# Queries and keys of the second head group as one product of quarters: seven jobs of 256 tokens

## The chip, the cores and the metric

One core of a Trainium2 chip runs the whole kernel as one program. The time is device microseconds of one execution. The engines are TensorE (PE; the loading of its weights is listed as PEld), VectorE (DVE), ScalarE (ACT), GpSimd (POOL) and SyncE (SP), whose queue issues nearly all DMAs. Each engine has its own stream of instructions; semaphores order the streams against each other.

## The reference

One layer of a decoder trunk on 512 tokens of width 1024, all in float32. After a norm, `u` is multiplied with one wide matrix `w_in` and split:

```python
u = rmsnorm(x, ln1_g[i])
proj = u @ w_in[i]
q, k, v, pool_in, z, xbc, dt_raw, gate_pre = jnp.split(proj, split_idx, axis=-1)
...
y_a = dilated_attention_mixer(q, k, v, rel_bias) @ w_a[i]
y_b = pool_mixer(pool_in, pool_w[i], pool_scale[i]) @ w_b[i]
y_c = ssd_mixer(z, xbc, dt_raw, ...) @ w_c[i]
gates = jax.nn.sigmoid(gate_pre + b_gate[i]).reshape(b, s, N_BRANCH, D_MODEL)
merged = gates[:, :, 0] * y_a + gates[:, :, 1] * y_b + gates[:, :, 2] * y_c
```

A gated feed-forward part and a last norm follow. The 18 attention heads of 64 columns are in three groups of six with dilations 1, 4 and 16, so queries and keys of one group are 384 columns each. The change concerns the queries and keys of the second group (group 1 in the code): `u` (512 x 1024) times a 1024 x 768 part of `w_in`.

## The kernel before

**Products in three parts.** A float32 factor is split into a high part (a cast to fp32r on ScalarE, `cast`, L195) and a low part (the difference to it on VectorE, `lows`, L215). `mm3` (L234) adds three products in PSUM: high x high, high x low, low x high. `uh` and `ul` are the parts of `u`, laid out with the 1024 inner columns on 8 x 128 partitions and the 512 tokens along the free axis.

**Jobs.** All work on TensorE is a list of `Job`s that `program()` yields in order. A job has one piece of weights and a body that issues its matmuls. While job n is issued, `prepare` puts the low part of job n+1's weights on VectorE, the cast of job n+2's on ScalarE (in two halves, each put in by the next `step()` of a body) and the load of job n+3's on SP's queue. There are two buffers for loaded weights (`wraw`), three for high parts (`whp`), two for low parts (`wlp`). The order of TensorE, ScalarE, VectorE and GpSimd is the order in which the code issues; SP's queue is ordered by the scheduler. `step()` also moves side work on: items of attention, of the scan and of the splits that wait in lists, one piece per step.

**PSUM.** Eight tiles of 128 x 512 float32, four under `MM`, four under `SM`, given out in turn.

**Products of quarters.** `sevens` and `sevens_down` compute a 2 x 2 block product with seven block products in place of eight, on sums and differences of quarters. `v_pair` (used for the values of groups 1 and 2) takes `u` by halves of the tokens and by even and odd inner blocks (`side_u`, with sums made by `sums_of_u`), and the weights by even and odd inner blocks and by left and right 384 columns. Its jobs have 24 matmuls of 384 columns (L234, tile `pb`), two tiles per job, each read out by an operation of its own. Differences of weights are made on VectorE by `diff` (L339), either after a job's low part (`then`) or just ahead of its cast (`form`).

**Queries and keys.** `qk_jobs(g)` has three jobs of 48 matmuls, each with 128 query and 128 key columns; a chunk is 24 matmuls of 512 tokens into a fresh `pqk` tile. ScalarE reads the query tile (L639), VectorE the key tile (L641).

**Order around the change.** `program()` runs `v_pair`, with the second branch's gate jobs 0 to 3 ahead of it, then `qk_jobs(1)`, then puts the attention items of group 1 on the list (`attend(1)`), then the gate chunks 4 to 7 (`SPLIT` is 4; two chunks of 24 matmuls per job, tile `pa`; the sigmoid is at L1085, the product at L1087), then the twelve chunks of xBC (L830, L834). The values' quarters are written to their places by 32 small DMAs on SP (L624).

Of the kernel before, what the change touches and what calls it, by code (L numbers as in the profile page):

```python
# [10 lines left out]
F32 = mybir.dt.float32  # L11
F32R = mybir.dt.float32r
AF = mybir.ActivationFunctionType
OP = mybir.AluOpType
AX = mybir.AxisListType

P = 128
S = 512
# [14 lines left out]
C_Q, C_K, C_V = 0, AW, 2 * AW  # L33
# [50 lines left out]
def trunk(ctx: ExitStack, tc, out, x, rel_bias, ln1_g, w_in, b_gate, w_a, pool_w, pool_scale, w_b,  # L84
# [3 lines left out]
    act, dve, pool, pe, sp = nc.scalar, nc.vector, nc.gpsimd, nc.tensor, nc.sync  # L88

    x, w_in, w_a, w_b, w_c, w_o = x[0], w_in[0], w_a[0], w_b[0], w_c[0], w_o[0]  # L90
# [10 lines left out]
    ypool = ctx.enter_context(tc.tile_pool(name="ypool", bufs=2))  # L101
# [6 lines left out]
    def T(name, dt=F32, shape=(P, S)):  # L108
        return big.tile(list(shape), dt, name=name, tag="t")

    def MM(name):
        return psum.tile([P, S], F32, name=name, tag="mm")
# [15 lines left out]
    def fill(items):  # L128

        for it in items:  # L130
            at = next((i for i, w in enumerate(waiting) if w is FREE), None)
            if at is None:
                waiting.append(it)
            else:
                waiting[at] = it
# [3 lines left out]
    def flush():  # L139
        todo = second[:]  # L140
        second.clear()
        for f in todo:
            f()
# [6 lines left out]
    def advance(it, phase):  # L150
        for at in it:
            if at is None or at > phase:
                return at
        running.remove(it)

    def step():
        flush()
        if waiting:
            running.append(iter(waiting.pop(0)))
        now = [(it, 0) for it in running]  # L160
        for phase in (0, ROWS, WHOLE):
            now = [(it, advance(it, phase) if at == phase else at) for it, at in now]

    def after(n, it):
        for _ in range(n):
            yield
        yield from it
# [57 lines left out]
    def wsrc(w, k0, k1, c0, c1):  # L225
        return w[k0 * P:k1 * P, c0:c1].rearrange("(k p) c -> p k c", p=P)

    def mm3(ps, wh, wl, xh, xl, ks, first=True, last=True, flip=False, again=False):

        n, total = 0, 3 * len(ks)  # L230
        for a, b in ((wh, xh), (wh, xl), (wl, xh)):
            for k in ks:
                l, r = (b(k), a(k)) if flip else (a(k), b(k))
                pe.matmul(ps, l, r, start=first and n == 0, stop=last and n == total - 1,  # L234
                          skip_group_check=again)
                n += 1

    def chunk_a(ps, ws, j, xh, xl, ks, lo=0, hi=S, k0=0):
        wh, wl = ws
        mm3(ps[:, lo:hi], lambda k: wh[:, k0 + k, j * P:(j + 1) * P],  # L240
            lambda k: wl[:, k0 + k, j * P:(j + 1) * P],
            lambda k: xh(k)[:, lo:hi], lambda k: xl(k)[:, lo:hi], ks)

    def chunk_a2(ps, ws, j, xh, xl):

        wh, wl = ws
        for k0 in (0, 4):
            mm3(ps, lambda k: wh[:, k, j * P:(j + 1) * P], lambda k: wl[:, k, j * P:(j + 1) * P],
                xh, xl, range(k0, k0 + 4), k0 == 0, k0 == 4)
            if k0 == 0:  # L250
                step()
# [86 lines left out]
    def diff(out, a, b):  # L338
        dve.tensor_tensor(out, a, b, OP.subtract)  # L339
        return out  # L340
# [70 lines left out]
    def side_u(j):  # L411
        if j in QUARTER:
            two, half = QUARTER[j]
            return [(uh[:, 2 * p + two, half], ul[:, 2 * p + two, half]) for p in range(4)]
        return [US[j, p] for p in range(4)]
# [151 lines left out]
    def perm(ap, g):  # L567
        return ap if g == 0 else ap.rearrange("p (j r) -> p r j", r=4)

    def grouped(ap, g):  # L570

        return ap.rearrange("p (r j) -> p r j", r=4)[:, :, ::-1]

    def blocked(ap, g):
        return ap.rearrange("p (r j) -> p r j", r=4) if g == 0 else perm(ap, g)

    def plain(ap, g):
        return ap if g == 0 else ap.rearrange("p (r j) -> p r j", r=4)

    dtr = cpool.tile([P, 4, SH], F32, name="dtr")  # L580
    V, QK, OT, NM, LS = {}, {}, {}, {}, {}
# [46 lines left out]
    def qk_jobs(g):  # L628
        for i in range(3):
            def body(ws, i=i):  # L630
                for j, which in enumerate("qk"):
                    ps = MM("pqk")
                    if g == 2 and i >= 3 - MORE:
                        chunk_a2(ps, ws, j, uhk, ulk)
                    else:
                        chunk_a(ps, ws, j, uhk, ulk, range(KD))
                    t = T(f"{which}{g}")
                    if which == "q":
                        act.mul(grouped(t, g), blocked(ps, g), 0.125)  # L639
                    else:  # L640
                        dve.tensor_copy(plain(t, g), perm(ps, g))  # L641
                    QK[which, g, i] = t
                    step()
            cq, ck = C_Q + 384 * g + i * P, C_K + 384 * g + i * P
            yield Job([wsrc(w_in, 0, KD, cq, cq + P), wsrc(w_in, 0, KD, ck, ck + P)], KD, 256, body)

    def attend(g):
        nm, ls = both[:, :, :HEADS], both[:, :, 32:]
# [172 lines left out]
    XS, YT, Y = {}, {}, {}  # L821
# [259 lines left out]
    def gate_jobs(b, lo=0, hi=8):  # L1081
        def evac(m, ps):
            s = SG[b, lo + m] = T("sg")
            o = o_bg + 8 * b + lo + m
            act.activation(s, ps, AF.Sigmoid, bias=col[:, o:o + 1])  # L1085
            if b == 1:
                dve.tensor_tensor(MG[lo + m], MG[lo + m], s, OP.mult)  # L1087

        return jobs_a(w_in, C_GATE + b * D + lo * P, hi - lo, uhk, ulk, KD, evac)
# [305 lines left out]
    def program():  # L1395
        yield from jobs_a(w_in, C_POOL, 8, uhk, ulk, KD, pool_evac)
        yield Call(lambda: waiting.append(rows_of_bias()))
        yield from v_jobs(0)
        yield from qk_jobs(0)
        yield from pool_out_job()  # L1400
        yield Call(lambda: attend(0))
        yield Call(lambda: waiting.insert(3, ssd_prep()))
        for i, job in enumerate(branch_jobs(1, w_b, YB, 8, more=range(7))):
            if i == 3:
                yield Call(lambda: running.extend(after(p, sums_of_u(p)) for p in range(4)))
            yield job
        load, pair = v_pair()
        yield Call(load)
        yield from gate_jobs(1, 0, SPLIT)
        yield from pair  # L1410
        yield from qk_jobs(1)
        yield Call(lambda: attend(1))
        yield from gate_jobs(1, SPLIT)
        yield from jobs_a(w_in, C_XBC, 12, uhk, ulk, KD, xbc_evac)
        yield Call(ssd_start)
        yield from qk_jobs(2)
        yield Call(lambda: attend(2))
        yield Call(lambda: fill([after(2, combine())]))
        yield from gate_jobs(0)
        many = {"a": branch_jobs(0, w_a, AO, 3), "g": gate_jobs(2),  # L1420
                "Z": z_jobs(0), "z": z_jobs(1)}
        for token in MIX:
            if token in many:
                yield next(many[token])
            else:
                yield Call(lambda i=int(token): waiting.append(y_norm(i)))
        yield Call(finish)
        yield from branch_jobs(2, w_c, YT, 8, last=True)
        yield Call(load_x1)
        for pair in range(2):  # L1430
            for h in range(2):
                yield from wo_jobs(pair, h)
            if pair == 0:
                yield Call(ff_cols)
        first, between, _ = sevens_down(0)
        second_, last_, opened = sevens_down(1, keep=True)
        extra = {EARLY + i: between[w] for i, w in enumerate(
            ("two", "one", "five", "three", "six", "seven", "four"))}
        extra.update({LATE + i: last_[w] for i, w in enumerate(("two", "one", "five", "six"))})
        for i, job in enumerate(up_jobs()):  # L1440
            yield job
            if i == EARLY - 3:
                yield Call(first)
            if i == LATE - 1:
                yield Call(second_)
            if i in extra:
                yield extra[i]
        yield Call(lambda: fin.setdefault("g", grow(final_g)))
        yield Call(finish)
        yield from down(last_, opened)  # L1450
# [79 lines left out]
    banks = [SM("uT") for _ in range(4)]  # L1530
# [7 lines left out]
    for tb in range(2):  # L1538
        s0, s1, v, sq, r, rt = (small(n, [P, 1]) for n in ("s0", "s1", "v", "sq", "r", "rt"))
# [22 lines left out]
    parts = lows(weights[1], 2)  # L1562


    r = rstd_of(ss, 2, D)
    for tb in (2, 3):
        for h in range(2):
            t = xin[tb, h]
# [65 lines left out]
SPLIT = 4  # L1634
# [33 lines left out]
```

## Time and profile before

| | |
|---|---|
| median of 3 runs | 1036.35 us (1036.2 to 1037.03) |
| the profiled execution, its own time | 1036.32 us |
| span of the profile | 1034.5 us |
| seven value jobs of groups 1 and 2 (168 matmuls of 384) | 29.14 us |
| queries and keys of group 1 (144 matmuls of 512) | 32.68 us |
| one gate chunk (24 matmuls of 512), the first after them | 5.44 us |

The page of the profile gives the span, each engine's busy time and the granted clock of TensorE. The chain of waits is followed back from the last instruction: at each step to what released it. In its view by time each row has a start, a length, an engine, the tile it writes, a line, and a count. In the timeline, rows have a start, a length, the engine and the operation with its tiles; a bracket at the end gives idle time of the engine ahead of it and what ended that. In the views by tile and by line, durations are nanoseconds (least/median/most, or the mean).

### The profile page before, as it was taken

The page shows a single profiled execution, that of the slowest core. Times are in us where ns is not written, and L with a number is a line of the kernel's source. Part 1 is how long each engine was busy: PE and PEld are TensorE (multiplying, and loading weights), DVE is VectorE, ACT ScalarE, POOL GpSimd, SP SyncE. Part 2 cuts the span into 40 slices and gives each one's busy share as a digit, 9 for nine tenths or more (in the row PEclk, how much of TensorE's full clock was granted, in tenths as well). Part 3 has the DMA queues.
Part 4 walks back from the last instruction along what each step waited for, and adds up shares of the span by engine and source line. Part 5 has one row for each costly group of instructions (what it writes and reads, how often), then busy time and mean ns, then how long its engine had stood idle before and what let it go on. Part 6 is the DMA issues. An engine that isn't in the chain of part 4 may idle for free.

```text
span 1034.5 us, 13089 instructions
## 1 busy us (share of the span) xinstructions
PE 1024.3 (99%) x5204; PEld 859.9 (83%) x5204; DVE 676.0 (65%) x907; ACT 473.8 (46%) x765; POOL 149.2 (14%) x125
## 2 busy tenths in 40 slices
PE   9999999999999999999999999999999999999997
PEld 9998878898888878888888888898888888888885
DVE  5553566684356658766768756766778677666775
ACT  6432554452464354567455324545444443453342
POOL 2770000000000004210153501101111001111120
PEclk9999999999999999999999999999999999999999
DMA  8344312026222345541254525443223324323142
GB/s 279 124 127 139 108 55 75 31 62 203 82 82 82 88 132 127 144 133 57 76 154 139 187 82 203 167 143 123 82 92 124 111 82 163 122 82 122 61 143 82
DMA packets 119068, 120.76 MB, mean 117 GB/s; under 512 B 5315, under 2 KB 101382, under 8 KB 119007
## 3 DMA queue, kind: packets, MB, share of 16 engines
q1 hardware_dynamic: 118415, 119.07, 35.9%
q8 instruction: 41, 0.67, 0.3%
q10 hardware_dynamic: 592, 0.86, 0.2%
q14 instruction: 20, 0.16, 0.0%
HBM read 116.12 MB, written 2.22 MB: 114 GB/s over the span
## 4 chain that ended last, share of the span: by engine, by line
PE 97%; DVE 1%; ACT 1%; DMA 1%; issue 0%; ACTq 0%; DVEq 0%
PE pa L234 35%; PE pu L234 22%; PE pb L234 11%; PE pqk L234 9%; PE p L234 8%; PE pa L1519 2%; PE ps L670 1%; PE pu L1326 1%; PE ppw L234 1%; PE pt L698 1%; PE po L711 1%; PE py L996 1%; DMA xin<-in_x_dram 1%; PE pyo L1003 1%; PE pst L982 0%; PE pxs L950 0%
## 5 line engine op out<-in xcount | busy, mean ns | idle before, releaser
L215 DVE TENSOR_TENSOR wl<-raw,wh 128x2048 fp32r<-128x2048 f32 (+3 forms) x95 | 218.4, 2301 | 46.9 <-ACT wh L195 39.2
L195 ACT CAST wh<-raw 128x1024 fp32r<-128x1024 f32 (+3 forms) x188 | 189.3, 1026 | 60.7 <-DVE raw L339 29.7
L1187 DVE SCALAR_TENSOR_TENSOR hc<-pu,fcol,hc 128x510 f32<-128x510 f32 x88 | 65.8, 748 | 61.1 <-ACT hc L1184 59.5
L234 PE MATMUL pa<-uh,wh 128*128 128x512 f32 x384 | 98.5, 398 | 0.0
L234 PE MATMUL pa<-ul,wh 128*128 128x512 f32 x384 | 94.9, 389 | 0.0
L234 PE MATMUL pa<-uh,wl 128*128 128x512 f32 x384 | 94.9, 389 | 0.0
L234 PEld LDWEIGHTS pa<-ul,wh 128*128 128x128 f32 x384 | 72.1, 188 | 15.2
L234 PEld LDWEIGHTS pa<-uh,wl 128*128 128x128 f32 x384 | 72.1, 188 | 15.0
L234 PE MATMUL pu<-uh,wl 128*128 128x512 f32 (+1 forms) x352 | 83.6, 380 | 0.0
L234 PE MATMUL pu<-uh,wh 128*128 128x512 f32 (+1 forms) x352 | 83.6, 379 | 0.0
L234 PE MATMUL pu<-ul,wh 128*128 128x512 f32 (+1 forms) x352 | 83.5, 379 | 0.0
L234 PEld LDWEIGHTS pa<-uh,wh 128*128 128x128 f32 x384 | 70.3, 188 | 14.7 <-issue 0.7
L234 PEld LDWEIGHTS pu<-uh,wl 128*128 128x128 f32 x352 | 64.1, 188 | 12.7 <-DVE wl L215 0.3
L234 PEld LDWEIGHTS pu<-ul,wh 128*128 128x128 f32 x352 | 64.2, 188 | 12.5
L234 PEld LDWEIGHTS pu<-uh,wh 128*128 128x128 f32 x352 | 64.1, 188 | 12.4
L1192 POOL TENSOR_TENSOR hc<-hc 128x512 f32<-128x512 f32 x22 | 30.4, 1384 | 278.9 <-DVE hc L1187 243.9
L1184 ACT ACTIVATE hc<-pu,fcol,fcol 128x512 f32<-128x512 f32 x40 | 31.2, 780 | 82.3 <-PE pu L234 82.0
L958 POOL TENSOR_TENSOR xd<-xc,dec 128x512 f32<-128x512 f32 x6 | 6.4, 1062 | 334.1 <-DVE xc L952 334.1
L1085 ACT ACTIVATE sg<-pa,col 128x512 f32<-128x512 f32 x24 | 16.5, 688 | 55.3 <-PE pa L234 48.6
L691 ACT ACTIVATE sb<-sb,both 128x128 f32<-128x128 f32 (+1 forms) x72 | 30.1, 418 | 23.5 <-DVE both L688 13.4
L234 PE MATMUL pqk<-uh,wh 128*128 128x512 f32 x144 | 36.9, 394 | 0.0
L234 PE MATMUL pqk<-ul,wh 128*128 128x512 f32 x144 | 36.3, 389 | 0.0
(352 smaller groups left out, 1793.5 us busy)
## 6 DMA issues: line engine op xcount, KB each, us to landing
raw<-in_w_in_dram SPq DMA_DIRECT2D x25, 1024.0 KB
raw<-in_ffn_w_up_dram SPq DMA_DIRECT2D x22, 1024.0 KB
raw<-in_ffn_w_down_dram SPq DMA_DIRECT2D x11, 1024.0 KB
raw<-in_w_in_dram SPq DMA_DIRECT2D x20, 512.0 KB
raw<-in_w_o_dram SPq DMA_DIRECT2D x8, 1024.0 KB
raw<-in_w_b_dram SPq DMA_DIRECT2D x4, 1024.0 KB
al<-ad SPq DMA_DIRECT2D x16, 256.0 KB
w<-in_ffn_w_down_dram SPq DMA_DIRECT2D x4, 1024.0 KB
```

What stands on the lines that cost most here:

```text
L195: act.copy(job.high[:, :, o], job.raw[:, :, o])
L215: (eng or dve).tensor_tensor(l[:, :, o], job.raw[:, :, o], h[:, :, o].bitcast(F32), OP.subtract)
L234: pe.matmul(ps, l, r, start=first and n == 0, stop=last and n == total - 1, skip_group_check=again)
L670: pe.matmul(pss[i][:, o:o + w * P], q[r, n * P:(n + 1) * P], k[r, kb * P:(kb + w) * P], start=True, stop=True)
L691: act.activation(sb[:, off:off + w * P], sb[:, off:off + w * P], AF.Exp, bias=nm[:, n, h:h + 1], accum_out=ls[:, n, h:h + 1])
L698: pe.transpose(pt[:, o:o + P], sb[:, o:o + P], eye)
L711: pe.matmul(po[DH * hh:DH * hh + DH, n * P:(n + 1) * P], V[g, kb + i][:, (2 * cc + hh) * DH:(2 * cc + hh + 1) * DH], probs[2 * cc + hh, mb ...
L1085: act.activation(s, ps, AF.Sigmoid, bias=col[:, o:o + 1])
L1184: act.activation(t, ps, AF.Identity, bias=ff["c1"][:, ff["b"] + m:ff["b"] + m + 1], scale=fw(2, m))
L1187: dve.scalar_tensor_tensor(t[:, sh:], ps[:, :S - sh], fw(k, m), t[:, sh:], OP.mult, OP.add)
L1192: pool.tensor_tensor(a, a, t, OP.mult)
L1519: pe.matmul(first[2 * n + j][:, lo:hi], a[:, k, j * P:(j + 1) * P], b[:, k, lo:hi], start=a is wh and b is uh and k == 0, stop=a is wl and ...
```

## The change

The three jobs of `qk_jobs(1)` go, and seven jobs of `qk_sevens(1)` come. The tokens are taken by halves of 256, the inner blocks by even and odd, and the columns by queries (h = 0) and keys (h = 1). Each job has three blocks of 128 columns; a block is 12 matmuls of 256 tokens. `at` puts block 0 and block 1 of a job in the two halves of one PSUM tile and block 2 in another. Sums of products are added in PSUM where they can be: p3 is added to p5's tiles (Z), and p6, p7 and p4 are added to p1's (X). After p6, after p7 and after p4 a part of the result is read out of X; p2 has tiles of its own (Y). `keep` copies p1 (times 0.125) and p5 aside, since they are needed later.

Six loads of 768 KB (128 x 4 x 384) replace three of 1024 KB: W[0] and W[1] stay in the two `xs` buffers, the others come through `wraw`, two of them twice. Four differences of weights (L339's `diff`) are made on VectorE. The sums of `u` made for `v_pair` are used again, so they are held longer.

In `program()` the loads of W are called after the sixth value job, gate chunks 4 and 5 come ahead of the queries and keys, and chunks 6 and 7 stay behind `attend(1)`.

```diff
@@ -643,6 +643,84 @@
                     step()
             cq, ck = C_Q + 384 * g + i * P, C_K + 384 * g + i * P
             yield Job([wsrc(w_in, 0, KD, cq, cq + P), wsrc(w_in, 0, KD, ck, ck + P)], KD, 256, body)
+
+    def qk_sevens(g):
+
+        cols = (C_Q + 384 * g, C_K + 384 * g)
+        q = lambda two, h: w_in[:, cols[h]:cols[h] + 384].rearrange(
+            "(k two p) c -> two p k c", two=2, p=P)[two]
+        W, X, Z, Y, r1, r5 = [], {}, {}, {}, {}, {}
+
+        def load():
+            for h in range(2):
+                W.append(ypool.tile([P, 4, S], F32, name="w3", tag="xs")[:, :, :384])
+                sp.dma_start(W[h], q(h, 1))
+
+        def at(banks, c):
+            return banks[c // 2][:, (c % 2) * 256:(c % 2) * 256 + 256]
+
+        def half(which, c, hi):
+            if (which, g, c) not in QK:
+                QK[which, g, c] = T(f"{which}{g}")
+            t = QK[which, g, c]
+            t = grouped(t, g) if which == "q" else plain(t, g)
+            return t[:, :, 64 * hi:64 * hi + 64]
+
+        def turned_(ap):
+            return ap.rearrange("p (j r) -> p r j", r=4)
+
+        def job(source, j, banks, name, use, form=None):
+            def body(ws):
+                wh, wl = ws
+                parts = side_u(j)
+                for c in range(3):
+                    fresh = name is not None
+                    if fresh and c % 2 == 0:
+                        banks[c // 2] = (MM if banks is Y else SM)(name)
+                    cs = slice(c * P, (c + 1) * P)
+                    mm3(at(banks, c), lambda k: wh[:, k, cs], lambda k: wl[:, k, cs],
+                        lambda k: parts[k][0], lambda k: parts[k][1], range(4),
+                        fresh and c % 2 == 0, True, again=not fresh or c % 2 == 1)
+                    use(c)
+                    if c != 1:
+                        step()
+            new = Job([source] if source is not None else [], 4, 384, body)
+            new.form = form
+            if source is None:
+                new.load = lambda: None
+            return new
+
+        def keep(r, name, banks, scale):
+            def use(c):
+                r[c] = T(name)[:, :256]
+                act.mul(r[c], at(banks, c), scale)
+            return use
+
+        def p2(c):
+            dve.scalar_tensor_tensor(half("q", c, 0), turned_(at(Y, c)), 0.125, turned_(r1[c]),
+                                     OP.mult, OP.add)
+
+        def p6(c):
+            r = T("r2")[:, :256]
+            act.copy(r, at(X, c))
+            dve.tensor_tensor(half("k", c, 0), turned_(at(Z, c)), turned_(r), OP.add)
+
+        def p7(c):
+            dve.tensor_tensor(half("k", c, 1), turned_(at(X, c)), turned_(r5[c]), OP.add)
+
+        def p4(c):
+            act.mul(half("q", c, 1), turned_(at(X, c)), 0.125)
+
+        one = job(q(0, 0), "A11", X, "p1", keep(r1, "r1", X, 0.125))
+        one.then = lambda: diff(W[0], W[0], one.raw)
+        two = job(q(1, 0), "A12", Y, "p2", p2)
+        five = job(None, 1, Z, "p5", keep(r5, "r5", Z, 1.0), lambda: W[0])
+        three = job(None, 4, Z, None, lambda c: None, lambda: W[1])
+        three.then = lambda: diff(W[1], W[1], W[0])
+        six = job(None, 2, X, None, p6, lambda: W[1])
+        seven = job(q(0, 0), 3, X, None, p7, lambda: diff(seven.raw, W[1], seven.raw))
+        four = job(q(1, 0), "A22", X, None, p4, lambda: diff(four.raw, four.raw, W[1]))
+        return load, [one, two, five, three, six, seven, four]
 
     def attend(g):
         nm, ls = both[:, :, :HEADS], both[:, :, 32:]
@@ -1407,10 +1485,15 @@
         load, pair = v_pair()
         yield Call(load)
         yield from gate_jobs(1, 0, SPLIT)
-        yield from pair
-        yield from qk_jobs(1)
+        load, keys = qk_sevens(1)
+        for i, job in enumerate(pair):
+            yield job
+            if i == 5:
+                yield Call(load)
+        yield from gate_jobs(1, SPLIT, SPLIT + 2)
+        yield from keys
         yield Call(lambda: attend(1))
-        yield from gate_jobs(1, SPLIT)
+        yield from gate_jobs(1, SPLIT + 2)
         yield from jobs_a(w_in, C_XBC, 12, uhk, ulk, KD, xbc_evac)
         yield Call(ssd_start)
         yield from qk_jobs(2)
```

## The prediction

> **What bounds the kernel now.** I read the page first, then the chain of waits in order of time around the changed stage, then who TensorE waited for.
>
> ```profile
> span 1034.5 us, 13089 instructions
> ...
> PE 1024.3 (99%) x5204; PEld 859.9 (83%) x5204; DVE 676.0 (65%) x907; ACT 473.8 (46%) x765; POOL 149.2 (14%) x125
> ...
> PEclk9999999999999999999999999999999999999999
> ```
>
> ```profile
> 206.56 29.14 PE pb L234 x168
> 235.71 32.68 PE pqk L234 x144
> 268.39 5.44 PE pa L234 x24
> ```
>
> ```profile
> PE pa L1476 <- DVE relb L523: 1.1, 1, 1.1
> PE pcb L927 <- ACT xcv L1015: 1.0, 1, 1.0
> ```
>
> TensorE is busy 99% of the span at full clock, and its longest wait anywhere is 1.1 us. The chain runs through the stage on TensorE alone: the values (pb, the seven jobs of v_pair), then queries and keys of group 1 (pqk), then a gate job. So a microsecond of TensorE taken out of the stage is a microsecond of the end, and any wait put in is paid in full. The stage to beat is 32.68 us.
>
> ```profile
> 206.40:235.50 29.10, 29.10 (x169) 29.09 (x168) 24.33 (x25) 13.64 (x20) 0.00 (x0) 1.00 0.21 64
> 235.50:268.20 32.70, 32.70 (x146) 27.08 (x145) 10.37 (x8) 9.79 (x11) 0.00 (x0) 1.00 0.59 185
> ```
>
> These two windows (columns: length, busy time of PE, PEld, DVE, ACT, POOL, then clock, DMA share, GB/s) compare a product of quarters with a plain one. In the first, VectorE is busy 24.33 of 29.10 us, in the second 10.37 of 32.70. The change makes the second stage like the first: cover is thin there.
>
> **What it saves on TensorE.** 144 matmuls of 512 tokens become 7 jobs x 3 blocks x 12 = 252 of 256 tokens. The price of the short ones is in the start of the kernel and of the up-projection, both with a new weight tile for each matmul:
>
> ```profile
> 12.08 9.59 PE pa L1519 x80
> ...
> 25.72 11.54 PE pa L1519 x96
> ...
> 675.86 3.83 PE pu L1326 x32
> ```
>
> 9.59/80, 11.54/96 and 3.83/32 are all 0.120 us, against 32.68/144 = 0.227. So a block of 12 takes 1.44 us, the 21 blocks 30.24, and the gain is 32.68 - 30.24 = **2.44 us**. That is the ceiling: the arithmetic falls by an eighth, but a short matmul costs more than half a long one.
>
> **What it adds: a wait after nearly every block.** Blocks 0 and 1 of a job lie in the two halves of one 128x512 PSUM tile, block 2 in another. In the changed kernel's list of instructions (it holds order and waits, no times) the first matmul of block 1 waits for the engine that empties block 0, though the halves don't overlap:
>
> ```
> p2 block 1: Matmult p2<-uh,wh 128x256 [waits DVE]
> p5 block 1: Matmult p5<-sah,wh 128x256 [waits Activation]
> p1 block 0 of seven: Matmult p1<-sbh,wh 128x256 [waits Activation]
> p1 block 1 of seven: Matmult p1<-sbh,wh 128x256 [waits DVE]
> ```
>
> By counting the semaphore's steps these are p2(0), the copy r5(0), the copy r2(1) and p7(0). Before, each chunk had a tile of its own, and in v_pair each of the two pieces. Six of the seven jobs read a result out between blocks 0 and 1 (three doesn't). What one such wait costs, no row shows; its parts do:
>
> ```profile
> L1519 PE MATMUL pa<-uh,wh x64: 278/283/365, 11.8 to 34.6; 128*128 128x256 f32 x64
> ```
> ```profile
> L1506 ACT ACTIVATE uh<-uT,g x16: 467/477/521, 10.8 to 25.3; 128x256 fp32r<-128x256 f32 x16
> L1507 DVE SCALAR_TENSOR_TENSOR ul<-uT,g,uh x16: 473/476/485, 11.3 to 26.1; 128x256 fp32r<-128x256 f32 x16
> ```
> ```profile
> L368 ACT COPY r<-pb x6: 481/482/482, 208.8 to 223.3; 128x384 f32<-128x384 f32 x6
> ```
> ```profile
> L699 DVE COPY sb<-pt 128x512 f32<-128x512 f32 x9 | 6.1, 680 | 0.0
> ...
> L716 DVE COPY o<-po 128x512 f32<-128x512 f32 x3 | 3.3, 1101 | 10.3 <-PE po L711 10.3
> ```
> ```profile
> 678.27 2.28 DVE L215 TENSOR_TENSOR wl<-raw,wh 128x2048 fp32r<-128x2048 f32 x1
> ...
> 680.61 1.98 PEld L1326 LDWEIGHTS pu<-uh,wl 128*128 128x128 f32 x16 [0.28 <-DVE wl L215]
> 680.61 2.18 PE L1326 MATMUL pu<-uh,wl 128*128 128x256 f32 x16
> ```
>
> A 256-token matmul lasts 0.283 us, so the last result is there 0.283 - 0.120 = 0.16 after its slot. VectorE ended at 678.27 + 2.28 = 680.55 and TensorE went on at 680.61: 0.05 for a semaphore each way. The 16 matmuls then took 2.18 instead of the 2.08 that 15 x 0.120 + 0.283 gives: 0.10 for starting anew. Emptying 256 columns on ScalarE lies between 0.32 (two thirds of the 384-column 0.482) and 0.48 (L1506); I take 0.40. On VectorE it lies between 0.42 and 0.77 (these reads and writes step through memory, and L716 with such steps takes 1101 against 680 in L699, times 1.6); I take 0.45, near L1507. One wait is 0.16 + 0.05 + 0.40 + 0.05 + 0.10 = **0.76 us**, and six are 4.6: already more than the gain.
>
> A rule of the Trainium skill (PSUM — Partial Sum Buffer, section on bank collisions) speaks against the change in the same way: two engines must not touch one bank of a partition together, and waits are to be set by bank, not by address. No run here shows such a collision. Set by address, the timetable below without the shared-tile waits would end 0.3 us under the old stage.
>
> **What the readers stand behind.** ScalarE and VectorE take their work in order, and between the readings stand the splits of later jobs' weights:
>
> ```profile
> L195 ACT CAST wh<-raw 128x768 fp32r<-128x768 f32 x12 | 9.7, 830 | 3.6 <-DVE raw L339 3.6
> ```
> ```profile
> 209.14 1.75 DVE L215 TENSOR_TENSOR wl<-w,wh 128x1536 fp32r<-128x1536 f32 x1
> 210.81 1.75 DVE L339 TENSOR_TENSOR w<-w,w 128x1536 f32<-128x1536 f32 x1
> ```
>
> Half a cast is 0.83 us (a new one each 0.75), a low part 1.75, a difference 1.75 (a new one each 1.67). Each sum of weights costs ScalarE nothing but makes its cast wait for VectorE. I laid the seven jobs out with these numbers, t = 0 at the first matmul of one:
> - one: r1(0) ends 2.04; block 1 starts at 2.19 instead of 1.44: **0.75**. The job ends at 5.07.
> - two: on VectorE five's low part stands ahead of p2(0). It needs the second half of five's cast, which ScalarE makes after r1(2) (5.67) until 6.43; low part to 8.23, p2(0) to 8.60, block 1 at 8.74 instead of 6.51: **2.23**.
> - five: **0.75**. It ends at 16.70.
> - three adds to p5's tile and waits for r5(1). Ahead of that on ScalarE is half of six's cast, which needs W[1] - W[0]: three's low part 12.2 to 13.95, difference to 15.62, cast to 16.50, r5(1) to 16.82: **0.27**.
> - six: its copy of block 0 stands behind seven's cast, which waits for seven's difference (21.52) and ends at 23.15; the copy ends 23.47, block 1 starts at 23.62 instead of 22.73: **0.89**.
> - seven writes the same tile: block 0 waits for copy r2(1), behind half of four's cast, behind four's difference (26.62). The copy ends 27.82; start 27.97 instead of 26.50: **1.47**. Block 1 waits for p7(0), behind four's low part (30.69); it ends 31.06, start 31.21 instead of 29.41: **1.80**.
> - four: **0.75**; the stage ends at 39.17.
>
> The waits sum to 8.91, and 30.24 + 8.91 = 39.15 (rounding apart) is 6.5 us over 32.68. **Sum: +8.9 - 2.4 = +6.5.** With both readings at their low bounds the same layout gives +5.9, with both at their high ones +8.1.
>
> **The rest, edit by edit.** The gate job put ahead of the keys is the same 48 matmuls (two of the 5.44 us pieces above), no change on TensorE. Taken out of the scores of group 1 it spares ScalarE some reloads:
>
> ```profile
> L1085 ACT ACT_TABLE_LOAD x10 | 12.8, 1283 | 0.2
> ```
>
> ScalarE isn't on the chain there, so nothing is gained; without the cover, two loads of 1.28 would be at stake. The scores of group 1 then meet two more chunks of xBC and two fewer gate chunks; before, their later items ran among xBC chunks without a wait of TensorE (the waits above name none), so I take zero, at worst a wait like pcb's 1.0. The loads: six of 768 KB for three of 1024 KB, plus where SP puts them. Its list has W[0] and W[1] before the scatter of the second values, one's weights after 8 of its pieces, two's after 16.
>
> ```profile
> 234.78 1.15 SPq L183 DMA_DIRECT2D raw<-in_w_in_dram  x2
> ...
> 236.03 5.54 SPq L624 DMA_DIRECT2D vr<-v  x8
> ...
> 238.64 1.05 ACT L195 CAST wh<-raw 128x1024 fp32r<-128x1024 f32 x1 [6.41 <-DMA raw<-in_w_in_dram]
> ...
> 241.67 1.15 SPq L183 DMA_DIRECT2D raw<-in_w_in_dram  x2
> ...
> 242.93 6.88 SPq L624 DMA_DIRECT2D vr<-v  x8
> ...
> 245.64 1.05 ACT L195 CAST wh<-raw 128x1024 fp32r<-128x1024 f32 x1 [3.60 <-DMA raw<-in_w_in_dram]
> ...
> 249.34 1.05 ACT L195 CAST wh<-raw 128x1024 fp32r<-128x1024 f32 x1 [2.65 <-DMA raw<-in_w_in_dram]
> ```
>
> one's weights take the place of the load at 234.78, needed by 246.6 now (235.71 + 2 x 5.44): hidden. two's take that of 241.67. The halves were there 4.0 us and some 7 us after their issues, so between 245.6 and 249.3; I take 246, as the load is 768 KB. Its cast stands ahead of r1(0) on ScalarE, with a gate's sigmoid between: the late bound moves r1(0) and adds 3.3 us (the layout gives +9.8). What comes later has 4 us and more to spare.
>
> **Rivals.**
> 1. Only the six plain waits stay and the queues behind them clear in time: 4.6 - 2.4 = +2.1, 1038.4. For it: v_pair ran with the same splits and not one wait. Against: there nothing of TensorE hung on the readers' places. 14%.
> 2. two's weights come late: +9.8, 1046.1. 14%.
> 3. The other side: the waits of block 1 are for the second half of the weights' cast (block 1 straddles the halves), long done, and the tiles bind nothing. Then the gain is the 2.44 less what the queues leave, 1033.9 to 1036.0; it decides if block 1 starts within 0.1 of block 0's last slot. Against: p2's wait is on VectorE, which makes no such half, and the semaphore counts. 7%.
> 4. The clock falls in the gaps. At the very start some matmuls took double:
>
> ```profile
> L1476 PE MATMUL pa<-ones x38: 274/275/579, 1.1 to 7.2; 128*128 128x128 f32 x38
> ```
>
> If the 17 blocks after two's long wait ran at double price, that is 17 x 1.44 = +24 on top, 1067. Every window quoted has clock 1.00, with gaps up to 1.1. 3%. The Trainium skill (TensorE: Matmul & The Clock Gate, Part 1) halves the clock after an idle window of about 3.4 us; my longest gap stays under it, and no trace here shows such a drop after a gap.
>
> **The numbers.** The profiled execution took 1036.32 (span 1034.5 and 1.8 around it), the median of the three is 1036.35, so the two stand for each other. 1036.32 + 6.5 = **1042.8**, 62%. The range 1039.5 to 1047.0 holds the two bounds (1042.2, 1044.4) and rival 2, and leaves out 1, 3 and 4 for the most part. A difference under 0.2% (2.07 us) can't be told from none: faster 4% (half of 3), the same 10% (the other half, and half of 1, which lies on the edge), slower 86%.
>
> **What would show it.** The stage from the first p1 to the last takes about 39 us, with TensorE idle about 9: nearly 0.75 before block 1 of one, five and four, over 2 before that of two, over 1 twice in seven. Releasers are ACT for p1 and p5, DVE for p2 and seven. Matmuls stay at 0.120. I am wrong if p1 to p4 run without gaps, if the gaps are all alike (rival 1), or if DMA is named as releaser.

## The result, and the profile after

| | before | changed |
|---|---|---|
| median | 1036.58 us (1036.2 to 1038.69, 6 runs) | 1046.53 us (1043.85 to 1048.87, 6 runs) |
| the profiled execution | 1036.32 us | 1045.46 us |
| span | 1034.5 us | 1043.5 us |

The changed kernel takes 1.0094 times as long, 95% interval [1.0075, 1.0113]. The page of its profile, the rows shown of before:

```profile
span 1043.5 us, 13347 instructions
...
PE 1024.7 (98%) x5312; PEld 864.2 (83%) x5312; DVE 690.7 (66%) x921; ACT 475.1 (46%) x778; POOL 149.4 (14%) x125
...
PEclk9999999999999999999999999999999999999999
```

TensorE's busy time didn't fall: 1024.7 against 1024.3. A matmul counts as busy until its end, which lies behind its slot, and every break in the stream shows such an end; so the eight breaks of the stage hide most of the gain of its arithmetic. Its idle time rose from 1034.5 - 1024.3 = 10.2 us to 1043.5 - 1024.7 = 18.8, and these 8.6 are most of the 9.0 by which the span is longer. The view of who TensorE waited for (total, times, longest) names them; tile `p` is that of the new jobs:

```profile
PE p L234 <- ACT r L696: 2.3, 3, 1.5
PE p L234 <- DVE q L700: 2.1, 1, 2.1
PE p L234 <- DVE k L709: 1.7, 1, 1.7
PE p L234 <- ACT r L705: 1.6, 2, 1.1
...
PE p L234 <- ACT q L712: 0.5, 1, 0.5
```

All are readings of PSUM (L696 p1 and p5, L700 p2, L705 p6, L709 p7, L712 p4). No weight and no DMA is named as releaser. The timeline of TensorE shows where; these are the first four matmuls of the stage, the first four of each block that waited, and the gate job behind:

```profile
247.26 0.64 PE L234 MATMUL p<-uh,wh 128*128 128x256 f32 x4
...
250.34 0.74 PE L234 MATMUL p<-uh,wh 128*128 128x256 f32 x4 [1.49 <-ACT r L696]
...
256.97 0.74 PE L234 MATMUL p<-uh,wh 128*128 128x256 f32 x4 [2.06 <-DVE q L700]
...
262.02 0.74 PE L234 MATMUL p<-sah,wh 128*128 128x256 f32 x4 [0.47 <-ACT r L696]
...
265.49 0.74 PE L234 MATMUL p<-sbh,wh 128*128 128x256 f32 x4 [0.34 <-ACT r L696]
...
271.97 0.74 PE L234 MATMUL p<-sah,wh 128*128 128x256 f32 x4 [0.46 <-ACT r L705]
...
276.25 0.74 PE L234 MATMUL p<-sbh,wh 128*128 128x256 f32 x4 [1.15 <-ACT r L705]
...
279.63 0.74 PE L234 MATMUL p<-sbh,wh 128*128 128x256 f32 x4 [1.69 <-DVE k L709]
...
284.67 0.74 PE L234 MATMUL p<-uh,wh 128*128 128x256 f32 x4 [0.47 <-ACT q L712]
...
287.64 2.00 PE L234 MATMUL pa<-uh,wh 128*128 128x512 f32 x8
```

The eight brackets sum to 8.13 us. The stage takes 287.64 - 247.26 = 40.38 us, against 32.68 before: +7.70. A bracket counts from the end of the last matmul, so a wait is 0.16 longer in slots: block 1 of one could have started at 247.26 + 1.44 = 248.70 and started at 250.34. The rest of the span's 9.0 us lies outside: the values start at 207.36 in this execution's chain of waits, 0.8 later than before, since the first tokens' load took 6.82 us in place of 6.06; and some 0.5 come after the stage, most of it behind the last product. The time outside the span, 1045.46 - 1043.5 = 1.96 us, is 0.14 longer too.

### The profile page after: what moved, and what is told of

It reads as the page before. It is cut to its first block, busy times and chain, and to the rows that moved or that the text cites. A ratio compares the mean times of both kernels' runs of the same rounds, so it can differ in the third digit from the quotient of the medians.

```text
span 1043.5 us, 13347 instructions
## 1 busy us (share of the span) xinstructions
PE 1024.7 (98%) x5312; PEld 864.2 (83%) x5312; DVE 690.7 (66%) x921; ACT 475.1 (46%) x778; POOL 149.4 (14%) x125
## 4 chain that ended last, share of the span: by engine, by line
PE 92%; DVE 3%; ACT 2%; DMA 1%; issue 1%; SPq 1%; ACTq 0%; DVEq 0%
PE pa L234 34%; PE pu L234 22%; PE pb L234 10%; PE p L234 9%; PE pqk L234 6%; PE pa L1602 2%; PE ps L748 1%; PE pu L1404 1%; DVE wl L215 1%; PE ppw L234 1%; PE pt L776 1%; PE po L789 1%; PE py L1074 1%; DMA xin<-in_x_dram 1%; ACT wh L195 1%
## 5 line engine op out<-in xcount | busy, mean ns | idle before, releaser
L1267 ACT ACTIVATE hc<-hc 128x512 f32<-128x512 f32 x22 | 13.9, 632 | 42.7 <-DVE hc L1265 42.6
L912 DVE SCALAR_TENSOR_TENSOR xs<-pa,col,xs 128x509 f32<-128x509 f32 (+2 forms) x24 | 18.0, 749 | 17.0 <-ACT xs L908 16.5
```

Source lines behind the costliest of these rows:

```text
L912: dve.scalar_tensor_tensor(t[:, sh:], ps[:, :S - sh], col[:, o_cw + 12 * k + m:o_cw + 12 * k + m + 1], t[:, sh:], OP.mult, OP.add)
L1267: act.activation(t, t, AF.Silu)
```

## The experiments

**A tile for each block, and the order of one difference.** Three kernels ran beside one that has only the reordering. In the first, each of the 21 blocks has a PSUM tile of its own:

```diff
-            return banks[c // 2][:, (c % 2) * 256:(c % 2) * 256 + 256]
+            return banks[c][:, :256]
...
-                    if fresh and c % 2 == 0:
-                        banks[c // 2] = (MM if banks is Y else SM)(name)
+                    if fresh:
+                        banks[c] = (SM if banks is X or (banks is Y and c == 0) else MM)(name)
...
-                        fresh and c % 2 == 0, True, again=not fresh or c % 2 == 1)
+                        fresh, True, again=not fresh)
```

> Each of the 21 blocks is added up in a PSUM tile of its own (nine tiles), all else as in the changed kernel. Theory 'shared tile': block 1 no longer waits for the reading of block 0; the same layout with the durations now measured gives a stage of 32.6 us (40.4 in the changed kernel) with 2.4 us of waits left, all in front of block 1 of seven and block 0 of four, so a time within 1 us of the kernel before (about 1036.5). Rival 'work of splitting': TensorE waits because VectorE and ScalarE have too much to do in 30 us, whatever the tiles; then most of the 9 us of waits stay and the time is over 1042.

It took 1037.74 us (1037.29 to 1041.0), ratio 1.0015 [1.0006, 1.0024] to the kernel before. Seven of the eight waits are gone, with the same weights split on the same engines. Left is one, in seven, behind the cast that waits for four's difference:

```profile
PE p L234 <- ACT r L705: 1.7, 1, 1.7
```

It stands ahead of block 1 of seven; the one that I expected ahead of block 0 of four didn't come. So the shared tile made the other waits, and the rival falls. The median is 1.2 us over the 1036.5 of the layout. The profile is that of the slowest execution, 1041.0, in which the clock fell twice, once at the start of the kernel and once in the stage ("the clock" below), so it can't say where the median's 1.2 lie. In the second kernel the one wait left is taken on too: the difference for four's weights goes ahead of seven's low part on VectorE, where it had idle time.

```diff
-        four = job(q(1, 0), "A22", X, None, p4, lambda: diff(four.raw, four.raw, W[1]))
-        return load, [one, two, five, three, six, seven, four]
+        four = job(q(1, 0), "A22", X, None, p4)
+        return load, [one, two, five, three, Call(lambda: diff(four.raw, four.raw, W[1])),
+                      six, seven, four]
```

> As before it with a tile for each block, and the difference for four's weights is made on VectorE ahead of seven's low part instead of behind it (it then lies in VectorE's idle time). Theory 'shared tile plus queue order': no wait is left, the stage takes 21 x 1.44 = 30.2 us, 2.4 under the kernel before: about 1034.1. Rival 'work of splitting': VectorE still needs some 23 us of the 30 and new waits of more than 1 us show elsewhere; no faster than 1036.

The chain of waits by time, around the stage:

```profile
236.51 10.92 PE pa L234 x48
247.44 30.31 PE p L234 x252
277.75 5.47 PE pa L234 x24
```

252 matmuls in 30.31 us, TensorE alone: 21 x 1.44 = 30.24 holds, 2.37 under the old stage. The time is 1035.36 us (1035.05 to 1035.68), ratio 0.9987 [0.9978, 0.9996]: faster than the kernel before by 1.3 us, not 2.4. The third kernel has the second edit alone, with the shared tiles:

> The changed kernel with its shared tiles, only the difference for four's weights is made ahead of seven's low part. Theory: of the two waits in seven (1.3 and 1.9 us) the first nearly goes to the plain 0.7, the second stays over 0.7; the layout gives 1.0 us less than the changed kernel (about 1045.5 for its 1046.5). If the queue order were the whole cause, both would go and the time fall by over 4 us.

1044.51 us (1043.25 to 1045.33). Its stage takes 38.70 us, from 247.10 to 285.80, against 39.69 in a second profile of the changed kernel (below): 1.0 less, as laid out, but by other waits than I wrote. In the changed kernel's list block 0 of seven waits behind four's cast; here that wait is gone and block 1's has grown:

```profile
277.78 0.74 PE L234 MATMUL p<-sbh,wh 128*128 128x256 f32 x4 [2.06 <-DVE k L709]
```

The other direction of the test also holds: the queue order alone is worth 1 us of the stage, the tiles, with that order, 38.70 - 30.31 = 8.4.

**The reordering alone.** The kernel before with two gate chunks ahead of the queries and keys:

```diff
         yield from pair
+        yield from gate_jobs(1, SPLIT, SPLIT + 2)
         yield from qk_jobs(1)
         yield Call(lambda: attend(1))
-        yield from gate_jobs(1, SPLIT)
+        yield from gate_jobs(1, SPLIT + 2)
```

> The kernel before with nothing but the gate job (chunks 4 and 5) moved ahead of the queries and keys of group 1. Theory: no cost and no gain, within 0.5 us of the kernel before (1036.5). Rival 'reordering costs': the items of group 1's attention now meet more xBC chunks and TensorE waits; over 1038.

1037.13 us (1036.21 to 1039.13), ratio 1.0004 [0.9995, 1.0013]. The stage took 32.64 us there, and TensorE waited nowhere in it or behind it that it had not before.

**The changed kernel again, more time for the loads, and a longer wait.**

> The changed kernel itself once more, for the spread of its executions (1043.85 to 1048.87 in six). Theory 'clock after a gap': its gaps of TensorE (up to 2.2 us) now and then halve the clock for some 3.4 us, as one of 1.75 us did in the kernel with a tile for each block, which costs 1.7 us each time; so the executions lie in steps of about 1.7 us over some 1044 to 1045.5, and the time rises as the mean granted clock falls: 1044 to 1046 at 0.998 or 0.999, about 1047 at 0.997, 1048.8 at 0.995. Rival 'late weights': the spread is from DMAs, and the clock is the same in slow and fast executions.

1045.5 us (1043.94 to 1047.11, 5 runs), ratio 1.0087 [1.0073, 1.0101]. This profile (the execution of 1044.26) has a stage of 39.69 us, from 246.66 to 286.35. Against the first, only the first wait differs:

```profile
249.05 0.74 PE L234 MATMUL p<-uh,wh 128*128 128x256 f32 x4 [0.80 <-ACT r L696]
```

Over both sets, the five executions at a mean clock of 0.999 took 1043.85 to 1045.99, the two at 0.995 1048.69 and 1048.87; of four at 0.997 three took 1046.64 to 1047.11, and the fourth is the 1044.26, whose clock was low only behind the last products. The time does not follow the mean clock alone: this execution has a lower mean than the five and is among the shortest. Next, all four gate chunks ahead of the keys:

```diff
-        yield from gate_jobs(1, SPLIT, SPLIT + 2)
+        yield from gate_jobs(1, SPLIT)
         yield from keys
         yield Call(lambda: attend(1))
-        yield from gate_jobs(1, SPLIT + 2)
```

> The changed kernel with all four remaining gate chunks ahead of the queries and keys (not two), so the loads have 10.9 us more. Theory: the wait of block 1 of one falls from 1.6 to the plain 0.7 (two's weights are there in time, so no cast holds up the reading of p1) and nothing else changes: 1.0 us less than the changed kernel, the seven other waits as they were. Rival 'late weights are the cause of the miss and the spread': over 3 us less and a spread under 1 us.

1044.7 us (1043.01 to 1045.38): 0.8 less than the 1045.5 of the changed kernel measured beside it. The wait of block 1 of one fell to the plain one, the others stayed:

```profile
259.75 0.74 PE L234 MATMUL p<-uh,wh 128*128 128x256 f32 x4 [0.47 <-ACT r L696]
...
266.38 1.03 PE L234 MATMUL p<-uh,wh 128*128 128x256 f32 x4 [2.06 <-DVE q L700]
...
272.92 0.74 PE L234 MATMUL p<-sah,wh 128*128 128x256 f32 x4 [0.47 <-ACT r L696]
```

The five executions still spread over 2.4 us (3.2 in the changed kernel's five), so the loads alone don't make the spread. Last, five copies into an unused tile on VectorE ahead of p2(0)'s reading, in the changed kernel:

```diff
         def p2(c):
+            if c == 0:
+                junk = T("junk")
+                for _ in range(5):
+                    dve.tensor_copy(junk, uh[:, 0, :].bitcast(F32))
```

> The changed kernel with five copies of 512 columns into an unused tile on VectorE ahead of the reading of p2(0), so the wait of block 1 of two grows from 2.2 us by what the copies take (2 to 3.5 us). Theory 'clock after a gap': a gap that long always halves the clock: the windows after it show a granted clock near 0.5 for about 3.4 us, and the time rises by the longer wait and 1.7 us more. Rival: the clock stays 1.00 and the time rises by the wait alone.

1048.47 us (1047.37 to 1049.77), 3.0 over the changed kernel. The wait grew by 4.24 - 2.06 = 2.18 us. Block 1 of one waited only 0.47 in this execution, with two gate chunks ahead as in the changed kernel, where it waited 1.49 and 0.80:

```profile
257.85 1.09 PE L234 MATMUL p<-uh,wh 128*128 128x256 f32 x4 [4.24 <-DVE q L704]
...
264.39 0.74 PE L234 MATMUL p<-sah,wh 128*128 128x256 f32 x4 [0.47 <-ACT r L696]
```

**The clock.** The windows of these kernels (length, busy times of PE, PEld, DVE, ACT, POOL, granted clock, DMA) have these rows below 1.00 ahead of the last product. First the kernel with a tile for each block, in the execution of 1041.0. It has two drops. One is at the start, behind a gap of 1.86 us that ended at 11.25: the transposes of the first tokens waited for a load of 7.30 us (6.06 in the profile before), and they and the 80 matmuls behind them took 3.23 and 10.00 us in place of 2.05 and 9.59, 1.6 more. The change touches nothing there. The other is behind the one gap of the stage, 1.75 us, that ended at 274.27:

```profile
10.00:12.00 2.00, 0.75 (x6) 0.75 (x7) 0.96 (x5) 2.00 (x3) 0.81 (x1) 0.97 1.08 393
12.00:14.00 2.00, 2.00 (x11) 2.00 (x11) 0.97 (x2) 1.28 (x4) 2.00 (x2) 0.50 1.05 396
14.00:16.00 2.00, 2.00 (x14) 2.00 (x13) 1.45 (x4) 1.62 (x6) 1.91 (x1) 0.68 0.35 106
...
274.00:276.00 2.00, 1.73 (x9) 1.73 (x10) 1.75 (x3) 1.23 (x3) 0.00 (x0) 0.68 0.93 328
276.00:278.00 2.00, 2.00 (x12) 2.00 (x11) 2.00 (x3) 1.56 (x2) 0.00 (x0) 0.50 0.00 0
278.00:280.00 2.00, 2.00 (x18) 2.00 (x18) 1.25 (x3) 0.44 (x1) 0.00 (x0) 0.97 0.85 243
```

The kernel with four gate chunks ahead, after the gap that ended at 266.38:

```profile
266.00:268.00 2.00, 1.62 (x8) 1.62 (x9) 0.32 (x1) 0.00 (x0) 0.00 (x0) 0.66 0.00 0
268.00:270.00 2.00, 2.00 (x12) 2.00 (x11) 0.62 (x1) 0.00 (x0) 0.00 (x0) 0.50 0.03 8
270.00:272.00 2.00, 2.00 (x18) 2.00 (x18) 0.96 (x2) 0.00 (x0) 0.00 (x0) 0.99 0.00 0
```

And the one with the longer wait, after 257.85:

```profile
258.00:260.00 2.00, 2.00 (x10) 2.00 (x11) 0.00 (x0) 0.00 (x0) 0.00 (x0) 0.50 0.00 0
260.00:262.00 2.00, 2.00 (x14) 2.00 (x13) 0.61 (x1) 0.00 (x0) 0.00 (x0) 0.64 0.00 0
```

The clock is at half for 3.4 us each time: in the case with four gate chunks 2 x (1 - 0.66) x 2 = 1.36, then 2.00 and 0.04. The price is read from block 1 of two to block 1 of five: 272.92 - 266.38 = 6.54, and 264.39 - 257.85 = 6.54, against 262.02 - 256.97 = 5.05 in the changed kernel's profile, where the same gap of 2.06 us left the clock alone. So 1.49 us each time, and of the 3.7 us by which the stage with the longer wait (43.05) passes 39.37 (that with four chunks ahead less its 1.49), 2.18 are the wait and 1.49 the clock; so the rival, a clock that stays at 1.00, is out in the one profile taken. That the longer executions of the changed kernel have such drops is not shown: neither of its two profiles caught one ahead of the last product, and the mean clock can't tell, since it also counts the time behind the last product (1044.26 has 0.997 without a drop ahead of that, 1044.92 of the kernel with four gate chunks 0.998 with one). What speaks for it is the spread. The two versions without a gap in the stage (own tiles and the earlier difference, with two and with four gate chunks ahead) spread over 0.63 and 1.25 us in 11 and 10 executions; the changed kernel's 11 spread over 5.0. Against it, the kernel before, which has no gap in its stage, also has single executions some 2 us above its median (1038.69, 1038.75), so part of the spread may come from elsewhere, the start for one.

**A last pair.** The kernel before was profiled once more beside the version with all three edits: own tiles, the earlier difference, four gate chunks ahead.

> The kernel before, profiled on the same chip as the next kernel. The kernel with own tiles and the earlier difference gained 2.4 us in its stage but 1.3 in its median. Theory 'first load and last store': the stage of queries and keys takes 32.7 us here and 30.3 there, all TensorE work between the first transposes and the last product is otherwise equal within 0.3 us, and what is missing lies before the first transposes or after the last product. Rival 'given back later': the stretch from the stage's end to the last product is over 0.8 us longer in the other kernel.

> A tile for each block, the difference for four's weights earlier, and all four gate chunks ahead of the queries and keys. Theory: the stage again takes 30.3 us without a wait, and the place of the two gate chunks costs nothing: the time is that of the same kernel with two chunks ahead (1035.4) within 0.5 us, 1 to 2.4 us under the kernel before. Rival 'late loads still cost': over 0.5 us faster than 1035.4.

The kernel before took 1036.87 us, the version 1034.31 (1033.48 to 1034.73), ratio 0.9975 [0.9965, 0.9984]: it beats both kernels. The two versions lie 1.05 us apart, which is the number of the rival (over 0.5) and not mine. Their chains of waits, first before, then the version (values, the stage, and VectorE's first small operation behind the last product):

```profile
207.17 29.14 PE pb L234 x168
236.31 32.68 PE pqk L234 x144
...
1029.79 0.17 DVE v L472
```

```profile
206.95 29.14 PE pb L234 x168
...
257.90 30.31 PE p L234 x252
...
1027.33 0.17 DVE v L472
```

From the values' start to that operation it is 1029.79 - 207.17 = 822.62 and 1027.33 - 206.95 = 820.38: 2.24 gained, nothing given back. In the profile of the version with two gate chunks ahead the same stretch is 1027.73 - 207.37 = 820.36, equal. So the 1.05 us between the medians of the two versions don't lie on TensorE between values and last product, and the "late loads" that I had written as the rival can't be it, though its number came. In the profiled executions 0.4 lies ahead of the values, 0.2 behind the products and 0.6 outside the span. The last part is in every execution: the time less the span is 2.18 to 2.31 us in the version with two gate chunks ahead, 1.66 to 1.82 in that with four, and 1.74 to 1.86 in the kernel before. So some 0.4 of the 1.1 us that the first of them gained less than its stage were lost outside the span. What makes it stays open.

## Why the prediction was right, and where it was off

The forecast was 1042.8 with a range to 1047.0; 1046.53 lies near its end. The direction, the place and the mechanism were right; the change was 3.7 us larger than the 6.5 forecast. Of these, 2.6 are seen in the profiled execution (1045.46, 9.14 over before): 1.2 in the stage, 0.8 ahead of the values, 0.5 behind the stage and 0.14 outside the span. The other 1.1 lie between this execution and the median and stay open. The range was drawn to 1047.0 for the late weights of rival 2, which came true in part; that it also held the shares at the start, behind the stage and in the spread, which the sum put at nothing, is luck.

- **The gain of 2.44.** Right: 30.31 us for the 252 matmuls once nothing holds them up.
- **A wait per shared tile, and the readers behind the splits.** Right: all eight waits came where they were laid out, behind the engines named, and six of them within 0.2 us. The forecast started block 1 or 0 late by (with 0.10 for starting anew; measured values are from the first timeline, with the 0.09 by which the block after a wait is longer):

| wait | forecast | measured |
|---|---|---|
| one, block 1 | 0.75 | 1.73 |
| two, block 1 | 2.23 | 2.31 |
| five, block 1 | 0.75 | 0.72 |
| three, block 0 | 0.27 | 0.59 |
| six, block 1 | 0.89 | 0.71 |
| seven, block 0 | 1.47 | 1.39 |
| seven, block 1 | 1.80 | 1.94 |
| four, block 1 | 0.75 | 0.72 |
| sum | 8.91 | 10.11 |

- **The mis-sized term inside the stage: two's weights.** I put their arrival at 246, with 249.3 as the late bound of rival 2. ScalarE and SP of the changed kernel:

```profile
242.30 0.53 SPq L183 DMA_DIRECT2D raw<-in_w_in_dram  x1
```
```profile
247.86 0.83 ACT L195 CAST wh<-raw 128x768 fp32r<-128x768 f32 x1 [4.23 <-DMA raw<-in_w_in_dram]
248.60 0.68 ACT L1163 ACTIVATE sg<-pa,col 128x512 f32<-128x512 f32 x1
249.18 0.82 ACT L195 CAST wh<-raw 128x768 fp32r<-128x768 f32 x1
249.90 0.38 ACT L696 ACTIVATE r<-p 128x256 f32<-128x256 f32 x1
```

The weights came between the two guesses, and p1's reading stood behind two half casts and a sigmoid: 1.0 us of the 1.2 that the waits are longer. This is one execution's size: in the second profile of the changed kernel the bracket is 0.80 in place of 1.49, and the eight waits sum to 9.4. Four gate chunks ahead brought it to the plain 0.47.
- **Readings on VectorE** were put at 0.45 and took 0.59 to 0.63 us (L700, L709), within the bounds 0.42 to 0.77. The 0.40 of ScalarE was 0.38.
- **The clock, rival 4: the argument against it did not hold.** I argued that the gaps stay too short, and priced a drop at 24 us for the whole rest of the stage. The profile before has no drop between its matmuls, but one 4.8 us behind its last product. In the runs a gap of 1.75 or 2.06 us was enough at times, and a drop lasts 3.4 us and costs 1.49. The changed kernel has brackets of 2.06, 1.69 and up to 1.49 us, so one or two such drops could lift some of its executions; no profile shows one, and how much of the median they make stays open.
- **Rival 1** (plain waits alone) is out: two, three and seven waited behind splits. **Rival 3** is out: with the tiles parted the waits went.
- **The gate chunks moved** cost nothing that TensorE shows, as put.

## What to carry to other kernels

Before a product is cut into smaller blocks, count the tiles: two blocks in one PSUM tile make TensorE wait for every reading between them (0.7 us here for 256 columns, and up to 2.3 where the reader's queue holds other work), while the short block itself saves 2.44/21 = 0.12. Give each block a tile and look at what stands ahead of each reader in its queue; here that turned +9.9 us into -1.3 with the same arithmetic, and into -2.4 with two more gate chunks ahead. A layout by hand from measured durations found seven of eight waits within about 0.3 us.

## What the runs showed of the hardware

A gap of TensorE of 2.06 us halved its granted clock for 3.4 us in one profile (four gate chunks ahead) and left it alone in three others, twice in one of them. In the profile with a tile for each block, gaps of 1.86 us at the start and 1.75 in the stage halved it; one of 1.67 at the start of another kernel (own tiles and the earlier difference) didn't. A gap of 4.24 us did it in the one profile taken. Behind the last product, where TensorE has nothing left to do, the eleven profiles show how much idle time went by until the clock was at half: from 2.0 us to 5.2. The first row is from own tiles with the earlier difference, whose last matmul ended at 1026.16, the second from four gate chunks ahead, 1036.20; the drops began at 1030.00 - 1.88 = 1028.12 and 1042.00 - 0.56 = 1041.44:

```profile
1028.00:1030.00 2.00, 0.00 (x0) 0.00 (x0) 1.18 (x5) 0.85 (x2) 0.00 (x0) 0.53 0.00 0
```
```profile
1040.00:1042.00 2.00, 0.00 (x0) 0.00 (x0) 0.00 (x0) 0.00 (x0) 0.00 (x0) 0.86 0.68 262
```

The Trainium skill (TensorE: Matmul & The Clock Gate, Part 1) has the clock fall after an idle window of about 3.4 us, and the window free-running. The length of the drop, 3.4 us, agrees, and so does the width of 2.0 to 5.2; but a gap, or an idle end, well under the window was enough here. That the same gap does it in one execution and not in another fits a window that runs freely. An estimate from these figures is that a little under 2 us of idle time within one window is enough; no run here varies the gap finely enough to show it.
